# A decoder layer on one core: a 256/320 column split, the pool's four products in one group, and memory heads first in the out-projection

## The chip, the cores and the metric

The kernel runs on one core of one Trainium2 chip. The metric is the device time of one launch in microseconds (us), as the median of several runs. The engines are TensorE (PE, with its weight loads shown apart as PEld), VectorE (DVE), ScalarE (ACT), GpSimd (POOL) and SyncE (SP), which here only issues transfers. Each engine works through its own queue in order; where one needs another's result it waits on a semaphore.

## The reference

One decoder layer for 256 tokens of width 2048, in fp32:

```python
h = rms_norm(x, g_mix)
z = h @ w_in        # columns: pool 512 | q latent 512 | kv latent 256 | rope key 64 | memory query 512
y_pool = pool_mixer(z_pool, w_pool, pool_scale)
y_mla  = mla_mixer(z_q, z_kv, z_kr, ...)              # 8 heads, causal
y_mem  = memory_cross_attention(z_mq, mem, ...)       # 4 heads over 256 memory rows
x = x + concat([y_pool, y_mla, y_mem]) @ w_o
x = x + conv_glu_ffn(rms_norm(x, g_ffn), ...)         # inner width 5632
```

`pool_mixer` takes, in four groups of 128 channels, a causal mean over the last 2, 4, 8 and 16 tokens less the token itself, multiplies each group by its own 128x128 matrix in `w_pool`, and scales the columns.

## The kernel before

Weights are fp32 in DRAM and come in through SP's queue in pieces of up to 128x2048 (tile `wr`, three buffers, `load_w`). Each piece is split on chip into a high part (`wh`, a cast on ACT, line 98) and a residue (`wl`, a subtraction on DVE, line 99); activations are split in the same way (`split_act`, the high part on ACT, the residue on DVE). A product then is three products of halves: high with high, low with high, high with low. Two forms are used: `gemm_t` and its like (weights stationary, results by feature) and `gemm_n` (activations stationary, results by token, lines 173 to 175 in the profile). Small products, transposes, scores and the pool's matrices stay in plain fp32.

PSUM is held as two pools of four banks each, `psm` for the large products and `psa` for all else.

The order in the first part of the layer:

1. Memory keys and values: `mem @ w_mem_kv` (16 steps of k, `gemm_n`, lines 317 to 328). The chip's transfer engines are full here.
2. Memory queries and rope key: `xg @ [w_mq | w_kr]`, 576 columns, 16 steps of k. For each step and each of two blocks of 128 tokens the 576 columns go to two PSUM banks (`pss`, from `ps_aux`), 288 to each; `mq_done` copies them out, to `t` (512 columns) and `kr` (64).
3. Latents of q and kv (`gemm_z`, six of them), with the four memory heads between them; their outputs lie in `catm`, the memory heads' part of the concatenation.
4. Four pool groups (`pool_in(0)` to `pool_in(3)`), with `q_up` and `kv_up` (up-projections of queries, keys and values) between them.
5. `pool_mix`: on DVE the sliding sums (tiles `s4`, four steps that double the window) and the differences (line 575, into `zp`); then for each group one fp32 product with its matrix (line 577, a `psa` bank each) and a `split_act` from that bank into `cat`, the pool's and the MLA heads' part. The matrices come by one transfer on ACT's queue into `wp`, one of three rotating tiles `tok` (line 564).
6. `q_up(1)` and `kv_up(1)`, the last queries and the values. Then the out-projection: for each of four column blocks `n`, `out_part(0, n, pss, c)` takes for c = 0 the pool features (`cat`, k 0 to 3) and for c = 1 the memory heads (`catm`), a second round takes the MLA heads. `mla_steps` is called after each k of the first round and lays the MLA heads between the products: rotated keys first (`rope_keys`: a product on DVE into a `tok`, eight transposes on PE at line 688, four copies on DVE at line 693 into `qkv`), then scores (line 703), softmax, transposes, values.
7. The GLU, 44 pairs (lines 145 to 158), and the down-projection (lines 866 to 967).

The code is written in the order above, but a scheduler orders each engine's queue, save for instructions under `keep`, which stay as written among themselves. It also sets the semaphores: where a tile is written again, the writer waits for the readers of what stood in it, and for a PSUM tile this holds for the bank as a whole, whichever columns are touched.

Of the kernel before, what the change touches and what calls it, by code (L numbers as in the profile page):

```python
# [11 lines left out]
F32 = mybir.dt.float32  # L12
# [6 lines left out]
P = 128  # L19
T = 256  # L20
NT = 2
# [39 lines left out]
def layer(ctx, tc, xT_d, xn_d, memT_d, vec_d, tab_d, w_z_d, w_mqkr_d, w_q_d, w_kv_d, w_mem_d, w_pool_d, w_o_d,  # L61
          w_g_d, w_u_d, w_dn_d, out_d):
    nc = tc.nc
# [15 lines left out]
    def ps_aux():  # L79
        return psa.tile([P, 512], F32, tag="a", name=nm("psa"))  # L80
# [7 lines left out]
    def keep(ins, on=True):  # L88

        return tc.keep_in_program_order(ins) if on else ins  # L90
# [69 lines left out]
    def gemm_n(pss, hi, lo, act, k0, first, last, kept=False, by_span=False):  # L160

        nk, n = hi.shape[1], hi.shape[2]
        nj = len(pss[0])
        w = n // nj
        order = [(tt, j) for tt in range(NT) for j in range(nj)]
        if by_span:
            order.sort(key=lambda x: x[1])
        for i in range(nk):
            for tt, j in order:
                xh = act[:, k0 + i, tt * P:(tt + 1) * P]  # L170
                xl = act[:, k0 + i, T + tt * P:T + (tt + 1) * P]
                ps, o = pss[tt][j], slice(j * w, (j + 1) * w)
                keep(nc.tensor.matmul(ps, xh, hi[:, i, o], start=first and i == 0, stop=False), kept)  # L173
                keep(nc.tensor.matmul(ps, xl, hi[:, i, o], start=False, stop=False), kept)  # L174
                keep(nc.tensor.matmul(ps, xh, lo[:, i, o], start=False, stop=last and i == nk - 1), kept)  # L175

    def split_act(dst, src, scale=None, kept=False):


        h, l = (dst[:, 0], dst[:, 1]) if len(dst.shape) == 3 else (dst[:, 0:T], dst[:, T:2 * T])  # L180
        if scale is None:
            nc.scalar.copy(h, src)
            nc.vector.tensor_tensor(l, src, h.bitcast(F32), op=ALU.subtract)
        else:
            keep(nc.scalar.activation(h, src, AF.Copy, scale=scale), kept)
            keep(nc.vector.scalar_tensor_tensor(l, src, scale, h.bitcast(F32), op0=ALU.mult, op1=ALU.subtract), kept)
# [4 lines left out]
    def v(name, i=0):  # L191
        o = VOFF[name] + i
        return vec[:, o:o + 1]
# [16 lines left out]
    mp = mix.enter_context(tc.tile_pool(name="mix", bufs=1))  # L210
# [12 lines left out]
    def tok():  # L223
        return mp.tile([P, 512], F32, tag="tok", name=nm("tok"), bufs=3)
# [67 lines left out]
    ps = ps_aux()  # L292
# [24 lines left out]
    pss = [[ps_main()[:] for _ in range(2)] for _ in range(NT)]  # L317
    for c in range(KD // 2):
# [5 lines left out]
        for i in range(2):  # L324
            k = 2 * c + i
# [3 lines left out]
        if c % 2:  # L329
            h = slice(2 * c - 2, 2 * c + 2)  # L330
# [5 lines left out]
    ps = ps_aux()  # L336
# [54 lines left out]
        nc.vector.tensor_tensor(rx2, rx, rx, op=ALU.mult)  # L391


    NH = 288
    kr = mp.tile([P, NT, ROPE], F32, name="kr")
    fmq = sm(NT * XH)
    fmq3 = fmq.rearrange("p (t h) -> p t h", h=XH)
    pss = [[ps_aux()[:, :NH] for _ in range(2)] for _ in range(NT)]
    for c in range(KD // 2):
        raw = load_w(w_mqkr_d[c], 2 * 576)  # L400
        for i in range(2):
# [15 lines left out]
    def mq_done():  # L417

        x_rstd()
        for tt in range(NT):  # L420
            t = tok()
            nc.scalar.copy(t[:, 0:NH], pss[tt][0][:, :NH])
            nc.scalar.copy(t[:, NH:512], pss[tt][1][:, :512 - NH])
            nc.scalar.copy(kr[:, tt, :], pss[tt][1][:, 512 - NH:NH])
            head_sq(fmq3[:, tt], t[:].rearrange("p (h d) -> p h d", d=XD))
            nc.vector.tensor_scalar(fmq3[:, tt], fmq3[:, tt], rx2[:, tt:tt + 1], None, op0=ALU.mult)
            to_features(mqT, t, tt, XH, gqk[:, 1:2])
        rsqrt_(fmq, fmq, 1.0 / XD)
        for tt in range(NT):
            nc.vector.tensor_scalar(fmq3[:, tt], fmq3[:, tt], rx[:, tt:tt + 1], 1.0 / math.sqrt(XD),  # L430
                                    op0=ALU.mult, op1=ALU.mult)


        dx = tok()
        for tt in range(NT):
            nc.vector.tensor_scalar(dx[:, tt * P:(tt + 1) * P], identf[:], rx[:, tt:tt + 1], None, op0=ALU.mult)
        ps = ps_aux()
        nc.tensor.matmul(ps[:, 0:T], ones[:], dx[:, 0:T], start=True, stop=True)
        nc.scalar.copy(rxb[:], ps[:, 0:T])
# [73 lines left out]
    zl = mp.tile([P, 6, 2 * T], F32R, name="zl")  # L513
# [4 lines left out]
    for m in range(6):  # L518
# [3 lines left out]
        ps = ps_main()  # L522
# [3 lines left out]
        a = zs[:, m // 4, :]  # L526
# [23 lines left out]


    zp = mp.tile([P, 4, T], F32, name="zp")
    def pool_in(g):
        raw = load_w(w_z_d[6 + g], STG)
        ps = ps_main()
        gemm_z(ps, raw, lambda k: xg[:, k, :], lambda: mem_steps(6 + g), False) if g == 0 else gemm_t(
            ps, raw, 0, lambda k: xg[:, k, :], range(KD))
        half_add(zp[:, g, :], ps)
        nc.vector.tensor_tensor(zp[:, g, :], zp[:, g, :], rxb[:], op=ALU.mult)


    def pool_mix():
        wp = tok()
        nc.scalar.dma_start(wp[:], w_pool_d)
        cur, w = zp, 1
        for g in range(4):
            nxt = s4()
            nc.vector.tensor_copy(nxt[:, g:4, 0:w], cur[:, g:4, 0:w])
            nc.vector.tensor_tensor(nxt[:, g:4, w:T], cur[:, g:4, w:T], cur[:, g:4, 0:T - w], op=ALU.add)
            cur = nxt  # L570
            w *= 2
            s = cur[:, g, :]
            e = TAB["edge"][0] + 16 * g
            nc.vector.tensor_tensor(s[:, 0:16], s[:, 0:16], tab[:, e:e + 16], op=ALU.mult)
            nc.vector.scalar_tensor_tensor(zp[:, g, :], s, 1.0 / w, zp[:, g, :], op0=ALU.mult, op1=ALU.subtract)
            ps = ps_aux()
            nc.tensor.matmul(ps[:, 0:T], wp[:, g * P:(g + 1) * P], zp[:, g, :], start=True, stop=True)
            split_act(cat[:, g, :], ps[:, 0:T], v("pool_scale", g))


    qkv = big.tile([P, 32, T], F32, tag="act", name="qkv")
# [49 lines left out]
    def kv_up(n):  # L631
        raw = load_w(w_kv_d[n], STG)
        for h in range(2):
            pss = [[ps_main()[:]] for _ in range(NT)]
            hi, lo = split_w(raw, h * HS, HS)
            gemm_n(pss, hi[:].rearrange("p (k n) -> p k n", n=512), lo.rearrange("p (k n) -> p k n", n=512),
                   zl, 4, True, True)
            for tt in range(NT):
                ps = pss[tt][0]
                p3 = ps.rearrange("p (h d) -> p h d", d=128)  # L640
                if n == 1:
                    nc.scalar.activation(vv[:, tt, 4 * h:4 * h + 4, :], p3, AF.Copy, scale=skv[:, tt:tt + 1])
                    continue
                t = tok()
                t3 = t[:].rearrange("p (h d) -> p h d", d=NOPE)
                o = slice(tt * H + 4 * h, tt * H + 4 * h + 4)
                nc.scalar.copy(t[:], ps)
                head_sq(fk[:, o], t3)
                nc.vector.tensor_scalar(fk[:, o], fk[:, o], skv2[:, tt:tt + 1], sskr[:, tt:tt + 1],
                                        op0=ALU.mult, op1=ALU.add)  # L650
                rsqrt_(fk[:, o], fk[:, o], 1.0 / QK)
                nc.vector.tensor_scalar(fkn[:, o], fk[:, o], skv[:, tt:tt + 1], None, op0=ALU.mult)
                nc.vector.tensor_scalar(fkr[:, o], fk[:, o], rx[:, tt:tt + 1], None, op0=ALU.mult)
                nc.vector.tensor_tensor(t3, t3, fkn[:, o].unsqueeze(2).to_broadcast([P, 4, NOPE]), op=ALU.mult)
                to_features(knT[:, 4 * h:4 * h + 4], t, tt, 4, None, "v")
# [21 lines left out]
                                op0=ALU.mult, op1=ALU.mult)  # L677

    kv_up(1)

    def rope_keys():
        for tt in range(NT):
# [43 lines left out]
        if done[0] == 4 * H + 4:  # L726
            mla_heads[H - 1].values()

    def out_part(i, n, pss, c):

        raw = load_w(w_o_d[i, n, c], STG)
        for h in range(2):
            hi, lo = split_w(raw, h * HS, HS)
            w = [t.rearrange("p (k n) -> p k n", n=NN) for t in (hi[:], lo)]
            k = c * 4 + h * 2
            act, k = (cat, 4 + k) if i else (cat, k) if k < 4 else (catm, k - 4)
            for r in range(2):
                kept = i == 0 or n + c == 0
                gemm_n(pss, *(t[:, r:r + 1] for t in w), act, k + r, c + h + r == 0, c + h + r == 3, kept)
                if kept:  # L740
                    mla_steps()

# [5 lines left out]

    for n in range(4):
        pss = [[ps_main()[:]] for _ in range(NT)]  # L750
        for c in range(2):
            out_part(0, n, pss, c)
        out_add(n, pss)


# [21 lines left out]
    for n in range(4):  # L777
        pss = [[ps_main()[:]] for _ in range(NT)]
        for c in range(2):
            out_part(1, n, pss, c)  # L780
        out_done(n, pss)
        if n:
            turn(n - 1)
# [268 lines left out]
```

## Time and profile before

| | us |
|---|---|
| median of 3 runs | 1003.43 (1003.19 to 1003.74) |
| profiled span, first to last instruction | 1001.9 |
| PE busy | 996.0 |
| DVE busy | 767.7 |
| ACT busy | 587.0 |

The profiled execution has a span of 1001.9 us; the page gives no other time for it, and the runs' median lies 1.5 us above, for what is around the span. A row of the timeline gives the start and the length in us, the engine, the line, the operation, the tiles written and read (buffer numbers left out) and how many were merged; in brackets the engine's idle time before it and what ended it. Lengths of matmuls overlap, so their pace is read from start to start. An fp32 product of the pool shows as two records.

By place in the span: memory keys and values up to 50 us, memory queries and rope key 50 to 77, latents and memory heads to about 126, pool groups and up-projections to 177, then the out-projection.

### The profile page before, as it was taken

Reading aid. Unit: us, or ns where it says so; the run is one execution under the profiler, and the core shown is the slowest. Engines: PE = TensorE matmul, PEld = TensorE weight load, DVE = VectorE, ACT = ScalarE, POOL = GpSimd, SP = SyncE. Lnnn points to the kernel's source line nnn. Section 1 sums busy time; section 2 is a strip of 40 time slices with the busy share of each in tenths; the row PEclk is TensorE's granted clock in tenths of the full one; section 3 lists DMA queues with packets and bytes.
Section 4 is the critical chain, followed back from the end, with each engine's and each line's share of the span. In section 5 each row is a group of like instructions: output and inputs, shape, how many; then the busy total and the mean of one; then the engine's idle time right before and its main releaser. Section 6 shows DMA issues by size and latency. Waiting matters only on the chain.

```text
span 1001.9 us, 14016 instructions
## 1 busy us (share of the span) xinstructions
PE 996.0 (99%) x5338; PEld 857.8 (86%) x5338; DVE 767.7 (77%) x1160; ACT 587.0 (59%) x859; POOL 18.5 (2%) x39
## 2 busy tenths in 40 slices
PE   9999999999999999999999999999999999999998
PEld 7898888888888888888888888888888888888886
DVE  6778689855677767677767677777677898998997
ACT  7678666544576556555655565555565665545652
POOL 1010000000000000000000000000000000010000
PEclk9999999999999999999999999999999999999999
DMA  9867443433664555555555555555556655585651
GB/s 357 293 241 281 156 175 138 167 128 132 232 224 169 199 188 202 174 205 188 191 200 192 197 180 199 194 184 208 189 191 223 240 207 178 203 305 199 216 205 43
DMA packets 31764, 200.17 MB, mean 200 GB/s; under 512 B 3664, under 2 KB 4176, under 8 KB 9808
## 3 DMA queue, kind: packets, MB, share of 16 engines
q1 hardware_dynamic: 28512, 189.04, 52.8%
q0 software_dynamic: 2752, 9.44, 2.7%
q8 instruction: 42, 0.69, 0.3%
q10 hardware_dynamic: 432, 0.79, 0.2%
q14 instruction: 26, 0.21, 0.1%
HBM read 195.06 MB, written 4.19 MB: 199 GB/s over the span
## 4 chain that ended last, share of the span: by engine, by line
PE 99%; DVE 0%; issue 0%
PE psm L156 47%; PE psm L175 5%; PE psm L173 5%; PE psm L174 5%; PE psm L140 4%; PE psa L882 4%; PE psm L882 4%; PE psa L880 4%; PE psa L881 4%; PE psm L880 4%; PE psm L881 4%; PE psm L124 3%; PE psa L703 1%; PE psa L173 1%; PE psa L175 1%; PE psa L174 1%
## 5 line engine op out<-in xcount | busy, mean ns | idle before, releaser
L99 DVE TENSOR_TENSOR wl<-wr,wh 128x1024 fp32r<-128x1024 f32 (+2 forms) x338 | 390.5, 1170 | 133.7 <-ACT wh L98 76.0
L98 ACT CAST wh<-wr 128x1024 fp32r<-128x1024 f32 (+2 forms) x338 | 339.5, 1009 | 139.3 <-PE psm L156 55.4
L156 PE MATMUL psm<-h,wh 128*128 128x512 f32 x1376 | 320.1, 390 | 0.0
L156 PEld LDWEIGHTS psm<-h,wh 128*128 128x128 f32 x1376 | 255.1, 188 | 51.2
L156 PEld LDWEIGHTS psm<-h,wl 128*128 128x128 f32 x1376 | 163.8, 188 | 3.3
L156 PE MATMUL psm<-h,wl 128*128 128x256 f32 x1376 | 164.5, 277 | 0.0
L98 ACT CAST wh<-dn 128x1024 fp32r<-128x1024 f32 (+1 forms) x66 | 66.0, 1008 | 75.5 <-PE psa L881 35.1
L99 DVE TENSOR_TENSOR wl<-dn,wh 128x1024 fp32r<-128x1024 f32 (+1 forms) x66 | 75.0, 1164 | 15.8 <-ACT wh L98 15.8
L817 ACT ACTIVATE gc<-g,vec 128x256 f32<-128x256 f32 x44 | 26.5, 602 | 93.4 <-DVE g L815 93.4
L819 DVE SCALAR_TENSOR_TENSOR gc<-g,vec,gc 128x255 f32<-128x255 f32 x88 | 42.5, 483 | 33.0 <-ACT gc L817 31.4
L173 PE MATMUL psm<-wh,cat 128*128 128x512 f32 x96 | 38.2, 398 | 0.0
L175 PE MATMUL psm<-wl,cat 128*128 128x512 f32 x96 | 37.4, 390 | 0.0
L174 PE MATMUL psm<-wh,cat 128*128 128x512 f32 x96 | 37.4, 389 | 0.0
L881 PE MATMUL psa<-wh,aT 128*128 128x512 f32 x88 | 34.3, 390 | 0.0
L880 PE MATMUL psa<-wh,aT 128*128 128x512 f32 x88 | 34.3, 389 | 0.0
L881 PE MATMUL psm<-wh,aT 128*128 128x512 f32 x88 | 34.3, 389 | 0.0
L880 PE MATMUL psm<-wh,aT 128*128 128x512 f32 x88 | 34.2, 389 | 0.0
L882 PE MATMUL psa<-wl,aT 128*128 128x512 f32 x88 | 33.9, 389 | 0.0
L882 PE MATMUL psm<-wl,aT 128*128 128x512 f32 x88 | 33.9, 389 | 0.0
L809 ACT COPY g<-psm 128x256 f32<-128x256 f32 x44 | 16.5, 375 | 27.7 <-PE psm L156 27.7
L881 PE MATMUL psm<-wh,aS 128*128 128x512 f32 x77 | 30.0, 390 | 0.0
L881 PE MATMUL psa<-wh,aS 128*128 128x512 f32 x77 | 30.0, 390 | 0.0
(238 smaller groups left out, 1424.2 us busy)
## 6 DMA issues: line engine op xcount, KB each, us to landing
wr<-in_w_g SPq DMA_DIRECT2D x44, 1024.0 KB, 4.8
wr<-in_w_u SPq DMA_DIRECT2D x44, 1024.0 KB, 4.8
wr<-in_w_dn SPq DMA_DIRECT2D x33, 1024.0 KB, 4.9
wr<-in_w_o SPq DMA_DIRECT2D x16, 1024.0 KB, 4.8
dn<-in_w_dn SPq DMA_DIRECT2D x11, 1024.0 KB, 4.8
wr<-in_w_z SPq DMA_DIRECT2D x10, 1024.0 KB, 6.7
wr<-in_w_mem SPq DMA_DIRECT2D x6, 1024.0 KB, 8.4
wr<-in_w_mqkr SPq DMA_DIRECT2D x8, 576.0 KB, 5.2
```

The lines of the kernel that those rows point to most:

```text
L98: keep(nc.scalar.copy(hi[:, c:e], raw[:, o + c:o + e]), kept)
L99: keep(nc.vector.tensor_tensor(lo[:, c:e], raw[:, o + c:o + e], hi[:, c:e].bitcast(F32), op=ALU.subtract), kept)
L124: keep(nc.tensor.matmul(out, w, m, start=first and c + i == 0 and not low, stop=last and c == cs[-1] and i == len(kc) - 1 and low == (c // ...
L140: keep(nc.tensor.matmul(o, parts[k // nk][low][:, i * P:(i + 1) * P], m, start=k == 0 and low == low_first, stop=k == KD - 1 and low != lo ...
L156: nc.tensor.matmul(o, parts[k // nk][low][:, i * P:(i + 1) * P], m, start=k == 0 and low == (s == 1), stop=k == KD - 1 and low == (s == 0) ...
L173: keep(nc.tensor.matmul(ps, xh, hi[:, i, o], start=first and i == 0, stop=False), kept)
L174: keep(nc.tensor.matmul(ps, xl, hi[:, i, o], start=False, stop=False), kept)
L175: keep(nc.tensor.matmul(ps, xh, lo[:, i, o], start=False, stop=last and i == nk - 1), kept)
L819: nc.vector.scalar_tensor_tensor(gc[:, d:T], g[:, 0:T - d], v(w, f), gc[:, d:T], op0=ALU.mult, op1=ALU.add)
L880: nc.tensor.matmul(ps, a[0], b[0], start=first, stop=False)
L881: nc.tensor.matmul(ps, a[1], b[0], start=False, stop=False)
L882: nc.tensor.matmul(ps, a[0], b[1], start=False, stop=last)
```

## The change

- The 576 columns go as 256 and 320 instead of twice 288; `gemm_n` takes the widths from the PSUM tiles. The copies in `mq_done` become 256 + 256 and 64.
- `pool_mix` keeps the sums and differences. The four products move into a function of their own, `pool_out`, that is called after `kv_up(1)`. Two products share one `psa` bank, in its two halves; the products are under `keep`, and so are those of the last half of `kv_up`. The matrices get a tile of their own, `wp`.
- In the first column block of the out-projection the memory heads (c = 1) come before the pool features (c = 0).

```diff
@@ gemm_n
-        w = n // nj
+        at = [0]
+        for p in pss[0]:
+            at.append(at[-1] + p.shape[1])
...
-                ps, o = pss[tt][j], slice(j * w, (j + 1) * w)
+                ps, o = pss[tt][j], slice(at[j], at[j + 1])
@@ memory queries and rope key
-    NH = 288
+    NH = (256, 320)
-    pss = [[ps_aux()[:, :NH] for _ in range(2)] for _ in range(NT)]
+    pss = [[ps_aux()[:, :n] for n in NH] for _ in range(NT)]
...
-            nc.scalar.copy(t[:, 0:NH], pss[tt][0][:, :NH])
-            nc.scalar.copy(t[:, NH:512], pss[tt][1][:, :512 - NH])
-            nc.scalar.copy(kr[:, tt, :], pss[tt][1][:, 512 - NH:NH])
+            nc.scalar.copy(t[:, 0:256], pss[tt][0])
+            nc.scalar.copy(t[:, 256:512], pss[tt][1][:, 0:256])
+            nc.scalar.copy(kr[:, tt, :], pss[tt][1][:, 256:320])
@@ pool
+    wp = mp.tile([P, 4 * P], F32, name="wp")
...
     def pool_mix():
-        wp = tok()
         nc.scalar.dma_start(wp[:], w_pool_d)
...
+    def pool_out():
+        for a in range(2):
             ps = ps_aux()
-            nc.tensor.matmul(ps[:, 0:T], wp[:, g * P:(g + 1) * P], zp[:, g, :], start=True, stop=True)
-            split_act(cat[:, g, :], ps[:, 0:T], v("pool_scale", g))
+            for g in (2 * a, 2 * a + 1):
+                o = ps[:, (g % 2) * T:(g % 2 + 1) * T]
+                keep(nc.tensor.matmul(o, wp[:, g * P:(g + 1) * P], zp[:, g, :], start=True, stop=True))
+                split_act(cat[:, g, :], o, v("pool_scale", g))
@@ kv_up
-                   zl, 4, True, True)
+                   zl, 4, True, True, n + h == 2)
...
     kv_up(1)
+    pool_out()
@@ out-projection
-    def out_part(i, n, pss, c):
+    def out_part(i, n, pss, c, o):
...
-                gemm_n(pss, *(t[:, r:r + 1] for t in w), act, k + r, c + h + r == 0, c + h + r == 3, kept)
+                gemm_n(pss, *(t[:, r:r + 1] for t in w), act, k + r, o + h + r == 0, o + h + r == 3, kept)
...
-        for c in range(2):
-            out_part(0, n, pss, c)
+        for o in range(2):
+            out_part(0, n, pss, o if n else 1 - o, o)
```

What the scheduler made of it is seen in the queues. PE at the end of `kv_up(1)`, before; names carry their buffer numbers, and the brackets name the semaphores that a row waits for (of DVE, of ACT, of PE itself, of a transfer). L577 are the pool's products, L266 transposes of queries, L173 to L175 products of `kv_up`.

```order
L173 MATMUL psm_301_1885<-wh_303_1887,zl_839 128x512 [waits Activation_49]
L577 MATMUL psa_280_1785<-zp_1289,tok_274_1760 128x256 [waits DVE_49]
L174 MATMUL psm_301_1885<-wh_303_1887,zl_839 128x512
L175 MATMUL psm_301_1885<-wl_304_1888,zl_839 128x512
L577 MATMUL psa_282_1794<-zp_1289,tok_274_1760 128x256 [waits DVE_49]
L266 MATMUL psa_292_1839<-identf_68,tok_290_1834 128x128 x4
L266 MATMUL psa_295_1850<-identf_68,tok_293_1845 128x128 [waits Activation_49]
L266 MATMUL psa_295_1850<-identf_68,tok_293_1845 128x128 x3
L173 MATMUL psm_302_1886<-wh_303_1887,zl_839 128x512
```

The third and fourth product stand between products of `kv_up`, each with its own bank. The same place after; lines are 2 to 8 higher, L584 are the pool's products, L696 the transposes of the rope keys, L175 to L177 the out-projection.

```order
L177 MATMUL psm_297_1870<-wl_299_1872,zl_839 128x512
L584 MATMUL psa_300_1889<-zp_1289,wp_1290 128x256 [waits DMAHW1_49,DVE_49]
L584 MATMUL psa_300_1889<-zp_1289,wp_1290 128x256 [waits DVE_49]
L584 MATMUL psa_301_1896<-zp_1289,wp_1290 128x256
L696 MATMUL psa_308_1919<-identf_68,tok_307_1917 128x128 [waits PE_49]
L696 MATMUL psa_308_1919<-identf_68,tok_307_1917 128x128 x3
L696 MATMUL psa_310_1928<-identf_68,tok_309_1926 128x128 [waits Activation_49]
L696 MATMUL psa_310_1928<-identf_68,tok_309_1926 128x128 x3
L584 MATMUL psa_301_1896<-zp_1289,wp_1290 128x256 [waits DVE_49]
L175 MATMUL psm_302_1903<-wh_305_1907,catm_838 128x512
```

The products stand behind `kv_up(1)`, with the eight transposes of the rope keys between the third and the fourth. The second product's wait on DVE is for the read of the first out of `psa_300`, the fourth's for the read of the third out of `psa_301`. The eight transposes of queries have moved ahead, between the products of `kv_up(1)`, four at a time.

DVE's queue around its reads of these banks (L186 before, L188 after), before:

```order
L671 TENSOR_TENSOR small_82<-small_82 128x16 [waits DVE_49]
L684 TENSOR_TENSOR tok_310_1919<-krr_1292,small_82 128x512 [waits DMAHW1_49,PE_49]
L186 SCALAR_TENSOR_TENSOR cat_1759<-psa_282_1794,vec_67,cat_1759 128x256 [waits Activation_49]
L673 TENSOR_SCALAR small_82<-small_82 128x8 [waits DVE_49]
L673 TENSOR_SCALAR small_82<-small_82 128x8
L684 TENSOR_TENSOR tok_312_1928<-krr_1292,small_82 128x512 [waits PE_49]
L206 RECIPROCAL small_82<-small_82 128x16 [waits Activation_49]
L99 TENSOR_TENSOR wl_315_1944<-wr_307_1907,wh_314_1943 128x1024
L676 TENSOR_SCALAR small_82<-small_82 128x8 [waits DVE_49]
L676 TENSOR_SCALAR small_82<-small_82 128x8
L99 TENSOR_TENSOR wl_324_1996<-wr_322_1993,wh_323_1995 128x1024 [waits DMAHW2_49]
```

and after:

```order
L692 TENSOR_TENSOR tok_309_1926<-krr_1293,small_82 128x512 [waits PE_49]
L99 TENSOR_TENSOR wl_312_1942<-wr_304_1905,wh_311_1941 128x1024
L208 RECIPROCAL small_82<-small_82 128x16 [waits Activation_49]
L99 TENSOR_TENSOR wl_321_1994<-wr_319_1991,wh_320_1993 128x1024 [waits DMAHW2_49,PE_49]
L683 TENSOR_SCALAR small_82<-small_82 128x8 [waits DVE_49]
L683 TENSOR_SCALAR small_82<-small_82 128x8
L188 SCALAR_TENSOR_TENSOR cat_1760<-psa_300_1889,vec_67,cat_1760 128x256 [waits Activation_49]
L99 TENSOR_TENSOR wl_328_2033<-wr_319_1991,wh_327_2032 128x1024 [waits PE_49,Activation_49]
L188 SCALAR_TENSOR_TENSOR cat_1760<-psa_300_1889,vec_67,cat_1760 128x256 [waits Activation_49]
L188 SCALAR_TENSOR_TENSOR cat_1760<-psa_301_1896,vec_67,cat_1760 128x256 [waits Activation_49]
L701 COPY qkv_1291<-psa_308_1919 64x4x128 [waits PE_49,Pool_49]
```

Before, three of the four reads stand ahead of the first row shown; after, all four stand behind the residues of two more weight pieces (`wl_312` and `wl_321`), with a third (`wl_328`) between the first and the second. The transfer of the matrices, which was the 183rd entry of ACT's queue, is now the ninth, ahead of a cast of memory weights.

More of the change, by code (lines that the diff above doesn't have):

```diff
@@ L779, in layer @@
         for c in range(2):
-            out_part(1, n, pss, c)
+            out_part(1, n, pss, c, c)
         out_done(n, pss)
```

## Prediction

> **What bounds the kernel now.** I read the page first, then the chain of waits by engine, then the timeline of TensorE and VectorE around the three places that the diff touches.
>
> ```profile
> span 1001.9 us, 14016 instructions
> PE 996.0 (99%) x5338; PEld 857.8 (86%) x5338; DVE 767.7 (77%) x1160; ACT 587.0 (59%) x859; POOL 18.5 (2%) x39
> ...
> PE 99%; DVE 0%; issue 0%
> ```
>
> TensorE (PE) is the bound from end to end: busy for 996.0 of 1001.9 us, and the chain that ended last is 99% PE. So two things alone can move the time: how long PE needs for its own products, and how long PE waits. Work on VectorE (DVE), ScalarE (ACT) or a queue counts only where it makes PE wait. The profiled span is 1001.9 us and the median of the runs 1003.43 us; I take the 1.5 us between them as fixed and add my difference to the median.
>
> **Part 1, the column split.** The stage of memory queries and rope key issues three groups of 64 matmuls of 288 columns, 192 in all, so 96 pairs of neighbouring pieces.
>
> ```profile
> L173 PE MATMUL psa<-wh,xg 128*128 128x288 f32 x64 | 19.0, 298 | 0.0
> ```
>
> The mean of 298 ns is from start to end and overlaps the next one; what counts is the distance from start to start.
>
> ```profile
> 53.02 0.29 PE L173 MATMUL psa<-wh,xg 128*128 128x288 f32 x1
> ...
> 56.62 0.29 PE L173 MATMUL psa<-wh,xg 128*128 128x288 f32 x1
> ...
> 402.81 3.83 PE L156 MATMUL psm<-h,wl 128*128 128x256 f32 x32
> 406.47 7.44 PE L156 MATMUL psm<-h,wh 128*128 128x512 f32 x32
> 413.75 3.82 PE L156 MATMUL psm<-h,wl 128*128 128x256 f32 x32
> ```
>
> The first two rows are 27 matmuls apart: 3.60/27 = 133.3 ns for 288 columns. The next three give (406.47 - 402.81)/32 = 114.4 ns for 256 and (413.75 - 406.47)/32 = 227.5 ns for 512. So 32 columns fewer than 288 save 18.9 ns, while 224 more cost 94.2, or 0.42 ns a column: there is a step just above 256. 320 columns have no row. On the line from 288 to 512 they take 133.3 + 32 x 0.42 = 146.8 ns, and the pair 261.2 instead of 266.7 ns: 5.5 ns x 96 = **0.53 us gained**, on PE's path, since PE runs there without gaps. The ends: 133.3 ns (if the step is a round-up that 320 still fits under) gives 1.8 us gained; 152.3 ns (if the 18.9 ns come back on the other piece) gives nothing. I take the line, since 288 is the nearest row. The copies out (288+224+64 columns, now 256+256+64) run on ACT beside PE's next products and cost nothing.
>
> [...]
>
> **Part 2, the pool's products.** Before, they lie one by one between the products of the value up-projection; each has a PSUM bank of its own.
>
> ```profile
> 163.19 0.39 PE L173 MATMUL psm<-wh,zl 128*128 128x512 f32 x1
> ...
> 168.18 0.39 PE L174 MATMUL psm<-wh,zl 128*128 128x512 f32 x1
> 168.60 0.67 PE L577 MATMUL psa<-zp,tok 128*128 128x256 f32 x2
> ...
> 169.34 0.39 PE L173 MATMUL psm<-wh,zl 128*128 128x512 f32 x1
> ...
> 170.26 0.59 PE L577 MATMUL psa<-zp,tok 128*128 128x256 f32 x2
> ...
> 170.93 0.39 PE L175 MATMUL psm<-wl,zl 128*128 128x512 f32 x1
> ...
> 174.11 1.03 PE L266 MATMUL psa<-identf,tok 128*128 128x128 f32 x8
> ...
> 175.22 0.39 PE L174 MATMUL psm<-wh,zl 128*128 128x512 f32 x1
> ...
> 177.03 0.39 PE L173 MATMUL psm<-wh,cat 128*128 128x512 f32 x1
> ```
>
> 163.19 to 168.18 holds 22 products: 0.227 us each. From 170.26 to 170.93 there is one product of the pool and one such product, so a pool product takes 0.67 - 0.23 = 0.44 us; eight transposes take 1.11 - 0.23 = 0.88 us (110 ns each). Back to back a product cannot be much under 0.43, so grouping by itself saves some 0.01 us each. The first product waits: 168.18 to 169.34 is 1.16, less 0.45 and 0.44 leaves 0.27 us, because its input ends late on DVE. Behind the up-projection that input is long ready, so this 0.27 us goes.
>
> What comes instead: two products now share one PSUM bank, and PE's second product waits until DVE has read the first out of it (the waits in the order above; `split_act` ends on DVE). So the question is when DVE gets there.
>
> ```profile
> 163.79 0.42 DVE L510 TENSOR_TENSOR zp<-hadd,psm 128x256 f32<-128x256 f32 x1 [0.90 <-ACT hadd L509]
> ...
> 165.92 1.22 DVE L99 TENSOR_TENSOR wl<-wr,wh 128x1024 fp32r<-128x1024 f32 x1
> 167.06 0.17 DVE L574 TENSOR_TENSOR s<-s,tab 128x16 f32<-128x16 f32 x1
> ...
> 168.08 0.42 DVE L575 SCALAR_TENSOR_TENSOR zp<-s,zp 128x256 f32<-128x256 f32 x1
> ...
> 170.63 0.48 DVE L186 SCALAR_TENSOR_TENSOR cat<-psa,vec,cat 128x256 fp32r<-128x256 f32 x1
> 171.03 0.17 DVE L574 TENSOR_TENSOR s<-s,tab 128x16 f32<-128x16 f32 x1
> ...
> 173.25 0.69 DVE L260 TENSOR_REDUCE small<-hsq 128x4 f32<-128x512 f32 x1
> 174.08 0.48 DVE L186 SCALAR_TENSOR_TENSOR cat<-psa,vec,cat 128x256 fp32r<-128x256 f32 x1
> ...
> 177.93 1.22 DVE L99 TENSOR_TENSOR wl<-wr,wh 128x1024 fp32r<-128x1024 f32 x1
> ...
> L186 DVE SCALAR_TENSOR_TENSOR cat<-psa,vec,cat 128x256 fp32r<-128x256 f32 x4 | 1.9, 484 | 0.1
> ```
>
> DVE is full here: from 163.79 to 177.93 it runs 14.14 us with one pause of 0.2 (before 174.08). After the change the same run stands ahead of the first `cat` operation, less four `cat` operations (0.40 each, 170.63 to 171.03), less the pause, plus one weight residue more, of 1.14 (165.92 to 167.06): 14.14 - 1.60 - 0.2 + 1.14 = 13.48. Its start, 163.79, hangs on PE and stays. So the first `cat` operation starts at 177.27 and ends, 0.48 later, at 177.75; PE starts 0.10 after such an end (168.08 + 0.42 to 168.60), at **177.85**.
>
> PE would be ready much sooner: 163.19 + 48 x 0.227 (the products up to the group) + 0.88 (the eight transposes of queries, now among them) + 0.43 (the first product) = 175.4. It waits **2.45 us**. From there: the second product, with the 0.07 that a product after a wait takes longer (the 0.67 of the first row against 0.59), to 178.35; the third to 178.8; the eight transposes of rope keys, pulled in here, to 179.68. The fourth product waits again, for DVE's read of the third: on DVE the residue for 1.14 follows at 177.67, to 178.8; ACT reads the second product from 178.6 (its end trails by 0.2, the 0.59 over the 0.43) for 0.48 (row below), DVE reads it from 179.1 for 0.40, then the third, to 180.0. PE goes on at 180.1: **0.42 us** more. The fourth product ends at 180.6, and the out-projection starts. Before, it started at 177.03 without the rope transposes, that is 177.91 with their 0.88. Part 2 costs 180.6 - 177.9 = **2.7 us**, its removed wait included. Its ends: 0.3 us gained if DVE were never late, and 3.2 if both queues run 0.25 later than I place them; the rows are those of this very stretch, so I keep 2.7.
>
> ```profile
> 169.58 0.48 ACT L185 ACTIVATE cat<-psa,vec 128x256 fp32r<-128x256 f32 x1
> ...
> 179.10 2.85 DVE L693 COPY qkv<-psa 64x512 f32<-64x512 f32 x4
> ...
> 182.22 0.39 PE L703 MATMUL psa<-qkv,mqT 128*128 128x128 f32 x2
> ```
>
> **Part 3, memory heads first.** PE does the same products in another order, at no cost. It is cover: pool features are then first needed 24 products (5.4 us) and the first scores after 180.6, and DVE has them by 182. Without it the first product at 180.6 would wait. The four rope copies (2.85 us, done at 181.95 for a score at 182.22) move too: they start at 180.0 with a 0.40 `cat` operation among them and end near 183.3, while the scores now come at 180.6 + 18 x 0.227 = 184.7. No wait follows.
>
> **The pool weights' transfer** moves from ACT's queue near 157 us to its ninth place at the start.
>
> ```profile
> 9.64 1.05 ACT L98 CAST wh<-wr 128x1024 fp32r<-128x1024 f32 x1 [0.97 <-DMA wr<-in_w_mem]
> ...
> 17.60 1.06 ACT L98 CAST wh<-wr 128x1024 fp32r<-128x1024 f32 x1 [0.62 <-DMA wr<-in_w_mem]
> ...
> 22.58 0.39 PE L173 MATMUL psm<-wh,mg 128*128 128x512 f32 x1
> ...
> 10.00:15.00 5.00, 4.96 (x22) 3.79 (x21) 3.76 (x5) 4.23 (x6) 0.68 (x1) 1.00 1.05 428
> ```
>
> The issue fits in ACT's 0.97 us of waiting before 9.64. The engines are full then (428 GB/s), so 256 KB delay what follows by 0.6 us; the cast at 17.60 feeds PE at 22.58, so 3.9 us lie between. Cost nothing; with that cover gone, 0.6.
>
> **Sum:** 2.7 - 0.53 = +2.15 us, so 1003.43 + 2.15 = **1005.6 us**. A change of 0.2% (2.0 us) is about what a measurement here can tell, so I stand hardly beyond it.
>
> **Rivals.**
> - Split without a gain (152 ns for 320): +2.7, 1006.1 us. For it: no row for 320; against: the step above 256. [...]
> - 320 at 288's price: 2.7 - 1.8 = +0.9, 1004.3 us. For it: a step exists; against: 512 lies on a slope.
> - Not slower: DVE reads the shared banks in time, so that no wait replaces the one removed. It decides at 175.4: if the first `cat` operation ends before that, 2.35 us sooner than I place it, 0.3 + 0.53 are gained: 1002.6 us. For it: today DVE reads the first product 2.0 us after its start (168.60 to 170.63) while PE goes on. Against it: ahead of that operation stand two residues and the rope keys' work, and DVE's run has no pause to skip.
> - The clock. At the start PE runs slow after idling:
>
> ```profile
> 1.05 4.30 PE L294 MATMUL psa<-ones 128*128 128x128 f32 x20 [1.05 <-DVE eps L201]
> ```
>
> 4.30/20 is 215 ns for 128 fp32 columns, where later ones take 110: half speed for about 4 us, though the granted clock reads 1.00. If 2.45 us of waiting brings that back, another 4.3 us at half speed add 2.1: 1007.7 us. Against it: no wait of this length is in the trace. [...]
>
> **How the numbers follow.** The forecast has 0.66, with a range of its own of 1005.1 to 1006.0, six tenths of it beyond +0.2%. Split without gain 0.12, 320 at 288's price 0.08, DVE in time 0.07, clock 0.07. Slower: 0.40 + 0.12 + 0.07 = 0.59. Same: 0.26 + 0.08 + most of 0.07, less a little for a gain beyond 0.2% that I cannot place: 0.37. Faster: 0.04. The range 1004.2 to 1006.4 holds the forecast and both prices of 320, and leaves out DVE in time and the clock (0.14).
>
> **What would show it.** Right: PE waits about 2.4 us before the second pool product and 0.4 before the fourth, both ended by the `cat` operation on DVE; 256 columns at 114 ns and 320 at 147 start to start; no wait at the first scores or the first pool features of the out-projection. Wrong: no PE wait in the group, 320 columns at 133 or over 152 ns, matmuls at half speed after the wait, or a new wait in the first 20 us.

## The result and the profile after

The changed kernel takes 1007.21 us (median of 7 runs, 1006.17 to 1007.90), the kernel before 1003.56 (7 runs, 1003.19 to 1003.88): ratio 1.0034, interval 1.0024 to 1.0043. It is slower by 3.65 us, where 2.15 were predicted. Its runs fall in two groups: three at 1006.17 to 1006.20 us with a mean granted clock of 0.999, and four at 1007.21 to 1007.90 with 0.997 to 0.998. The profiled execution is of the lower group: 1006.17 us with a span of 1004.4, so 1.8 us lie around the span. For the kernel before it is the same (runs of 1003.55 us have a span of 1001.8).

The page of the changed kernel:

```profile
span 1004.4 us, 14015 instructions
PE 996.2 (99%) x5338; PEld 858.4 (85%) x5338; DVE 767.0 (76%) x1160; ACT 586.9 (58%) x859; POOL 18.5 (2%) x39
...
PE 98%; DVE 1%; issue 0%; ACT 0%
```

PE has the same work (996.2 us against 996.0), and a per cent of the chain has gone from PE to DVE. The timeline of PE shows where (start, length, then the row's work; the bracket is idle time and what ended it):

```profile
174.89 0.60 PE L584 MATMUL psa<-zp,wp 128*128 128x256 f32 x2
177.67 1.13 PE L584 MATMUL psa<-zp,wp 128*128 128x256 f32 x4 [2.19 <-DVE cat L188]
178.64 1.04 PE L696 MATMUL psa<-identf,tok 128*128 128x128 f32 x8
179.89 0.70 PE L584 MATMUL psa<-zp,wp 128*128 128x256 f32 x2 [0.21 <-DVE cat L188]
180.24 0.58 PE L175 MATMUL psm<-wh,catm 128*128 128x512 f32 x1
```

The first pool product is through at 174.89 + 0.43 = 175.32, the second starts at 177.67: PE stands for 2.35 us. (The bracket says 2.19, since it counts from the modelled end of the product ahead, not from when the next could have started.) The eight transposes end at 178.64 + 8 x 0.11 = 179.52, and the fourth product waits 0.37 more. VectorE in the same place:

```profile
177.14 0.48 DVE L188 SCALAR_TENSOR_TENSOR cat<-psa,vec,cat 128x256 fp32r<-128x256 f32 x1
177.53 1.22 DVE L99 TENSOR_TENSOR wl<-wr,wh 128x1024 fp32r<-128x1024 f32 x1
178.92 0.92 DVE L188 SCALAR_TENSOR_TENSOR cat<-psa,vec,cat 128x256 fp32r<-128x256 f32 x2 [0.17 <-ACT cat L187]
```

The read of the first product ends at 177.62, and PE goes on 0.05 us later; the third product's read, behind a residue and the second product's, ends the second wait.

For the sum, landmarks of both kernels: the first product of the memory queries, the first one behind them, the first of the last query up-projection, the first of the GLU. Before (the third landmark, 163.19, stands in the prediction):

```profile
50.15 0.38 PE L173 MATMUL psa<-wh,xg 128*128 128x288 f32 x1
...
76.79 0.87 PE L140 MATMUL psm<-xg,wh 128*128 128x512 f32 x3
...
287.90 2.07 PE L124 MATMUL psm<-h,wh 128*128 128x512 f32 x8
```

After, with three rows of the split:

```profile
50.05 0.37 PE L175 MATMUL psa<-wh,xg 128*128 128x256 f32 x1
...
50.94 0.28 PE L175 MATMUL psa<-wh,xg 128*128 128x256 f32 x1
...
51.30 0.31 PE L175 MATMUL psa<-wh,xg 128*128 128x320 f32 x1
...
51.74 0.28 PE L175 MATMUL psa<-wh,xg 128*128 128x256 f32 x1
...
76.68 0.86 PE L140 MATMUL psm<-xg,wh 128*128 128x512 f32 x3
...
163.07 0.39 PE L175 MATMUL psm<-wh,zl 128*128 128x512 f32 x1
...
290.45 2.07 PE L124 MATMUL psm<-h,wh 128*128 128x512 f32 x8
```

The stage of memory queries lasts 26.63 us after and 26.64 before: the split gains nothing. From 163.07 to the GLU it is 127.38 us against 124.71: **+2.67 us**, all in the part of the pool's products. The rest of the span differs by less than 0.15. So the profiled execution, and the lower group of runs, is explained. What puts four of seven runs another 1.0 to 1.7 us higher does not show in this trace.

### The profile page after: what moved, and what is told of

Same layout as the page of the kernel before. It is cut to its first block, busy times and chain, and to the rows that moved or that the text cites. A ratio compares the mean times of both kernels' runs of the same rounds, so it can differ in the third digit from the quotient of the medians.

```text
span 1004.4 us, 14015 instructions
## 1 busy us (share of the span) xinstructions
PE 996.2 (99%) x5338; PEld 858.4 (85%) x5338; DVE 767.0 (76%) x1160; ACT 586.9 (58%) x859; POOL 18.5 (2%) x39
## 4 chain that ended last, share of the span: by engine, by line
PE 98%; DVE 1%; issue 0%; ACT 0%
PE psm L156 47%; PE psm L175 5%; PE psm L176 5%; PE psm L177 5%; PE psm L140 4%; PE psa L890 4%; PE psm L890 4%; PE psa L888 4%; PE psa L889 4%; PE psm L888 4%; PE psm L889 4%; PE psm L124 3%; PE psa L711 1%; PE psa L175 1%; PE psa L177 1%; PE psa L176 1%
## 5 line engine op out<-in xcount | busy, mean ns | idle before, releaser
L175 PE MATMUL psm<-wh,cat 128*128 128x512 f32 x96 | 38.1, 397 | 0.0
L177 PE MATMUL psm<-wl,cat 128*128 128x512 f32 x96 | 37.4, 390 | 0.0
```

## Experiments

The theory: the two waits for a shared PSUM bank cost 2.67 us in each run, and in some runs the idling also brings TensorE's clock down for a while. The rivals: another part of the change costs (the early transfer, the order, the split), or the upper group has nothing to do with the idling.

### A bank for each product

```diff
         for a in range(2):
-            ps = ps_aux()
             for g in (2 * a, 2 * a + 1):
-                o = ps[:, (g % 2) * T:(g % 2 + 1) * T]
+                o = ps_aux()[:, 0:T]
```

> The four pool products stay in one group behind the value up-projection, but each gets a PSUM bank of its own. Theory W (the loss is TensorE's two waits for the shared banks, and what the clock does after the longer one): both waits are gone, about 2.8 us of the profiled span with them; span 1001.6, runs at 1003.1 to 1003.4 us, all with the granted clock of the kernel before (1.000), none in a second cluster. Rival R (something else in the change costs, such as the early transfer, the split or the order): the waits go, but runs stay at 1004.4 or above, or still fall in two clusters 1.0 to 1.7 us apart.

Measured: 1003.54 us (11 runs, 1003.02 to 1003.70), one group; ratio to the kernel before 0.9999, interval 0.9990 to 1.0007. PE's timeline:

```profile
162.94 0.39 PE L175 MATMUL psm<-wh,zl 128*128 128x512 f32 x1
...
174.77 1.89 PE L583 MATMUL psa<-zp,wp 128*128 128x256 f32 x8
176.31 0.58 PE L175 MATMUL psm<-wh,catm 128*128 128x512 f32 x1
...
287.42 2.07 PE L124 MATMUL psm<-h,wh 128*128 128x512 f32 x8
```

All four products run without a pause, and both the waits and the upper group are gone, although the split, the early transfer, the group and the new order are all still there. The loss is therefore the shared banks. The trace gains 0.23 us on the kernel before from the up-projection to the GLU (124.48 against 124.71), about the wait of 0.27 that the prediction saw there. The runs do not show that gain: 1003.1 to 1003.4 us were expected, and the profiled run, at 1003.02, is the fastest of the eleven. This is the best version of the study, and it equals the kernel before.

### The even split put back

```diff
-    NH = (256, 320)
+    NH = (288, 288)
```

(with the copies of `mq_done` as before)

> The changed kernel with the columns split as before, 288 and 288; the rest of the change is kept. Theory P (start to start a product takes (columns + 32)/2.4 ns here, so that both splits cost the pair 266.7 ns): the stage of memory queries lasts as long as in the changed kernel within 0.1 us, spans 1004.4 and 1005.4 to 1006.1 as there, two clusters of runs as there. Rival (the step on record: 256 columns at 114.4 ns, 320 at 146.8): the stage is 0.53 us longer and spans begin at 1004.9.

Measured: 1006.79 us (5 runs: 1006.08, 1006.45, 1006.79, 1007.55, 1007.55), ratio 1.0033, interval 1.0020 to 1.0046, close to the changed kernel. Its stage of memory queries takes 26.65 us (50.18 to 76.83), against 26.63 with 256 and 320. Here the profiled execution fell in the upper group (span 1005.8), and its timeline shows what that is:

```profile
175.09 0.60 PE L584 MATMUL psa<-zp,wp 128*128 128x256 f32 x2
177.86 1.83 PE L584 MATMUL psa<-zp,wp 128*128 128x256 f32 x4 [2.18 <-DVE cat L188]
179.48 1.91 PE L696 MATMUL psa<-identf,tok 128*128 128x128 f32 x8
181.19 0.79 PE L584 MATMUL psa<-zp,wp 128*128 128x256 f32 x2
181.62 0.58 PE L175 MATMUL psm<-wh,catm 128*128 128x512 f32 x1
```

The same wait of 2.34 us, but what follows it is slow: the second and third product take 177.86 to 179.48, 1.62 us instead of 0.97 (177.67 to 178.64 above), and 179.48 to 181.19 is 214 ns for each of the eight transposes instead of 110. The wait before the fourth product is gone, because PE now comes later than VectorE. In windows (from and to, length, PE busy with its count, granted clock, DMA share, GB/s):

```profile
174.00:178.00 4.00, 1.82 (x9) 1.00 0.26 47
178.00:179.00 1.00, 1.00 (x3) 0.57 0.99 418
179.00:180.00 1.00, 1.00 (x5) 0.50 1.06 434
...
181.00:182.00 1.00, 1.00 (x5) 0.72 0.98 418
182.00:186.00 4.00, 4.00 (x19) 1.00 0.29 119
```

The granted clock is 0.50 from shortly after the wait until about 181.6. Against the changed kernel's profile this run is 1.21 us longer between the same landmarks (163.26 to 291.85).

A stretch of 3.41 us at half clock takes 1.7 of some 1005 us, or 0.0017, off the mean granted clock of a run. So that mean tells the groups apart: 0.999 or 1.000 below, 0.997 or 0.998 above. The run at 1006.79 us lies between the groups with 0.999, so it had no such stretch; what it lost is not shown.

### A shorter wait

ScalarE copies the first product of each bank to SBUF, and VectorE splits it from there:

```diff
+                if g % 2 == 0:
+                    nc.scalar.copy(spare[:, a, :], o)
+                    o = spare[:, a, :]
                 split_act(cat[:, g, :], o, v("pool_scale", g))
```

> The changed kernel, but the first product of each shared bank is first copied to SBUF by ScalarE and split from there, so that the bank comes free when ScalarE has read it instead of VectorE: TensorE's wait should be about 1.0 us instead of 2.35, and about 0.25 instead of 0.38. Theory W (a short wait costs its length alone, a wait beyond some 2 us sometimes brings the slow clock as well): 1.5 us less than the fast cluster of the changed kernel, 1004.5 to 1004.8 us, all runs with a clock of 0.999 or more and within 0.4 us. Rival C (any wait of a microsecond can bring the slow clock): two clusters, the upper at 1005.7 or more with a clock of 0.998.

Measured: 1004.48 us (11 runs, 1004.25 to 1004.74, where 1004.5 to 1004.8 were expected), one group, clock 0.999 or 1.000; ratio 1.0009, interval 1.0000 to 1.0018.

```profile
175.01 0.60 PE L586 MATMUL psa<-zp,wp 128*128 128x256 f32 x2
176.28 1.13 PE L586 MATMUL psa<-zp,wp 128*128 128x256 f32 x4 [0.67 <-ACT spare L588]
```

The wait is 176.28 - 175.44 = 0.84 us, and 0.84 is about what the runs are above those with a bank each (0.94). In these eleven runs a wait this short costs its length and no more.

### A longer wait

Six more copies of the first product out of its bank, on VectorE:

```diff
+                for _ in range(6 if g == 0 else 0):
+                    nc.vector.tensor_copy(spare[:], o)
                 split_act(cat[:, g, :], o, v("pool_scale", g))
```

> The changed kernel with six more copies of the first product out of its shared bank on VectorE (their result is not used), which lengthen TensorE's wait before the second product to about 6 us. Theory W (after so long a wait the products run at half speed for about 4 us): every run has the lower clock (0.997 or less), the trace shows products 454 ns apart instead of 227 behind the wait, and the time is 6.4 + 0.7 us of waits and some 1 to 2 us for the slow products above own banks: 1011.3 to 1012.5 us, in one cluster. Rival (the waiting is all; the lower clock of some runs has another cause): products 227 ns apart behind the wait and 1010.2 us.

Measured: 1012.79 us (4 runs, 1012.02 to 1013.56), clock 0.994 to 0.996 in all; ratio 1.0094, interval 1.0079 to 1.0110.

```profile
174.85 0.60 PE L586 MATMUL psa<-zp,wp 128*128 128x256 f32 x2
181.61 2.08 PE L586 MATMUL psa<-zp,wp 128*128 128x256 f32 x4 [6.16 <-DVE cat L188]
183.47 1.27 PE L700 MATMUL psa<-identf,tok 128*128 128x128 f32 x5
```

A wait of 6.33 us brings the half clock in all four runs, as their granted clock shows. In the profile the second and third pool products take 181.61 to 183.47, 1.86 us instead of 0.97. By the records of the clock (last section) it had begun already during the wait, at 178.48, and that part of it cost nothing. Two of the four runs lie above the range expected, by 0.6 and 1.1 us; no trace was kept of these, and why is open.

### The same delay without the idling

Five more products of 256 fp32 columns, with no use of their result, in the wait:

```diff
                 split_act(cat[:, g, :], o, v("pool_scale", g))
+                if g == 0:
+                    fill = ps_aux()[:, 0:T]
+                    for i in range(5):
+                        keep(nc.tensor.matmul(fill, wp[:, 0:P], zp[:, 0, :], start=True, stop=True))
```

> The changed kernel with five extra products of 256 fp32 columns laid into TensorE's long wait (their result is not used), 5 x 0.43 = 2.15 of its 2.35 us. The second pool product still cannot start before VectorE has read the first, so the delay is the same and only the idling is gone. Theory W (the upper cluster of the changed kernel is the half-speed clock that follows the idling): all runs in the lower cluster, 1006.0 to 1006.4 us, profiled span 1004.3, no stretch with a granted clock of 0.5 behind the wait. Rival (the upper cluster comes from elsewhere, or from the delay itself): runs at 1007.2 to 1007.9 remain.

Measured: 1006.35 us (9 runs, 1005.96 to 1006.49), one group; ratio 1.0025, interval 1.0015 to 1.0035.

```profile
174.72 0.60 PE L584 MATMUL psa<-zp,wp 128*128 128x256 f32 x2
175.15 2.32 PE L589 MATMUL psa<-zp,wp 128*128 128x256 f32 x10
177.50 1.13 PE L584 MATMUL psa<-zp,wp 128*128 128x256 f32 x4
...
179.72 0.70 PE L584 MATMUL psa<-zp,wp 128*128 128x256 f32 x2 [0.21 <-DVE cat L188]
```

The second product starts 2.35 us behind the end of the first as before (177.50 - 175.15), so the delay of the lower group stays, and the upper group is gone. Useless work on the engine that is the bound brings the median from 1007.21 to 1006.35 us. The upper group is the idling, and not the delay.

With one extra product instead of five (`range(1)`):

> As warm_wait with one extra product instead of five: the same delay, but TensorE idles 1.9 us instead of 2.35. The traces so far show the granted clock change only on a grid of 3.41 us (174.08 and 822.61 us at full clock are 51 and 241 of it), half clock after a grid cell with 2.34 us of idling, and none after a cell with about 2.0. Theory G (a cell must be idle for more than some 2.0 us): all runs at 1006.0 to 1006.4. Rival (about 1 to 1.9 us in a cell suffice): runs above 1007 remain, fewer than in the changed kernel.

Measured: 1006.27 us (10 runs, 1005.99 to 1006.40), one group; ratio 1.0026, interval 1.0016 to 1.0035.

```profile
175.57 0.59 PE L589 MATMUL psa<-zp,wp 128*128 128x256 f32 x2
177.92 1.13 PE L584 MATMUL psa<-zp,wp 128*128 128x256 f32 x4 [1.76 <-DVE cat L188]
```

The upper group is missing here too: 1.92 us of idling (177.92 - 176.00) brought it in none of ten runs, 2.35 us in four of seven.

### A wait of 3 us

As the longer wait, with `range(2 if g == 0 else 0)`:

> As wait_plus6 with two extra copies instead of six: TensorE idles about 3.1 us. Theory G: a cell of 3.41 us then holds more than 2.3 us of the idling in most positions of the grid, so most runs (at least 6 in 10) have the half-speed stretch: those at 1007.9 to 1008.6, the others at 1006.9. [...]

Measured: 1008.03 us (5 runs: 1007.19, 1007.87, 1008.03, 1008.17, 1008.48), ratio 1.0042, interval 1.0029 to 1.0055. In its profile the wait is 178.36 - 175.37 = 2.99 us:

```profile
174.94 0.60 PE L586 MATMUL psa<-zp,wp 128*128 128x256 f32 x2
178.36 1.13 PE L586 MATMUL psa<-zp,wp 128*128 128x256 f32 x4 [2.82 <-DVE cat L188]
179.33 1.56 PE L700 MATMUL psa<-identf,tok 128*128 128x128 f32 x8
180.68 1.12 PE L586 MATMUL psa<-zp,wp 128*128 128x256 f32 x2
181.24 0.99 PE L175 MATMUL psm<-wh,catm 128*128 128x512 f32 x1
```

The two products right behind the wait still run at full speed (0.97 us), and the clock falls only among the transposes (1.56 instead of 1.04 us), 1.3 us after PE went on. So it isn't set by when the wait ends. Four of five runs lie at 1007.87 or above, as the grid theory had it. None lies at 1006.9, where that theory put the runs without the stretch. The lowest, at 1007.19, is nearest to it and has a clock of 0.999, so it had no half-speed stretch; the other four have 0.997 or 0.998.

### Pool features first again

```diff
-            out_part(0, n, pss, o if n else 1 - o, o)
+            out_part(0, n, pss, o, o)
```

> The changed kernel with part 3 undone: the first column block of the out-projection takes the pool's features before the memory heads again. The step on record (memory heads first is cover; without it the first product of the out-projection would wait for the pool's features): a third wait of TensorE of 0.5 to 1.5 us behind the group, 1006.7 us and above even in the lower cluster. Rival N (by the rows of the changed kernel the first features are ready at 177.6 and the fourth group's, needed 18 products or 4.1 us after the start at 180.4, by 181.7): no wait, the same two clusters as the changed kernel, 1006.1 and 1007.2 to 1007.9.

Measured: 1007.28 us (5 runs: 1006.15, 1006.21, 1007.28, 1007.44, 1007.74), ratio 1.0032, interval 1.0020 to 1.0045. No third wait:

```profile
179.73 0.70 PE L584 MATMUL psa<-zp,wp 128*128 128x256 f32 x2 [0.21 <-DVE cat L188]
180.08 0.58 PE L175 MATMUL psm<-wh,cat 128*128 128x512 f32 x1
```

The order of the out-projection changes nothing that these five runs show, in the lower group or in the upper.

## Why the prediction was wrong, and where it was right

- **The direction and the main term were right.** Part 2 was put at +2.7 us and measured 2.67: a wait of 2.35 us (predicted 2.45) ended by the `cat` operation that starts at 177.14 (predicted 177.27), and one of 0.37 (0.42). Walking VectorE's queue op by op gave that. The first product behind each wait takes some 0.11 us longer (the second and third together 0.97 instead of 0.86), where I had 0.07; with that, 2.35 + 0.37 + 0.22 - 0.27 = 2.67. The removed wait of 0.27 us was real too: with a bank each, 0.23 comes back.
- **Part 1 was mis-sized: a gain of 0.01 us instead of 0.53.** 320 columns were placed well (146.8 predicted; 51.30 to 51.74 holds three, 146.7 ns each). 256 was not: 50.94 to 51.30 gives 120 ns, where I took 114.4 from the GLU. So the pair costs 266.7 ns in both splits, and the rival "split without a gain" holds, but at the other end: 256 was dear, not 320. The step above 256 that I read from two stages does not exist within this one. In it 120, 133.3 and 146.7 ns for 256, 288 and 320 columns lie on one line of 0.417 ns a column, so both pairs are equal. Why 256 columns take 114 ns in the GLU and 120 here was not tried.
- **The clock was the step that failed.** The sum put the half clock at nothing, and four of seven runs pay for it. With part 1 at nothing, the sum is 1003.56 + 2.67 = 1006.2 us, where the lower group lies; the median is a microsecond higher. I had this rival, with the right mechanism, and gave it 0.07, on the ground that no wait of this length was in the trace. Waits of 2.34 and 2.99 us were enough in the profiles of the even split and of the 3 us wait. Its size was taken too large as well: 2.1 us, from 4.3 us at half speed. It is 1.0 to 1.7: the stretch is 3.41 us, so 1.7 at most, and the 0.37 us wait for the fourth product vanishes in it. Of the 1.6 us between forecast and median, about 1.0 is the clock, 0.5 the split, and 0.1 the kernel before, which came out at 1003.56 instead of 1003.43. In which group the median of seven runs falls is chance: about half of the runs lie in each, and a median of 1006.2 us would have hidden this step.
- **Part 3 as cover was wrong without consequence.** I wrote that without memory heads first the first product would wait. The first features are ready by then, and the fourth group's are needed 18 products later; pool features first cost nothing (180.08 in that run's timeline, right behind the group).
- **The early transfer** cost nothing, as predicted: the stage behind the full transfer engines (1.04 of their time and 420 GB/s from 10 to 20 us) begins at 50.05 us against 50.15.
- **The span and the median**: both kernels have 1.8 us around the span. The 1.5 that I took compared an execution with the median of others; it did not enter the difference.

## What to carry to other kernels

Two products that share a PSUM bank tie TensorE to the reader of the first one, where, as here, the bank is guarded as a whole (the second product, in the other half, stood for 2.35 us). When that reader's queue is full, give each product its own bank: here that gave back all that the sharing had cost (1003.54 against 1007.21 us), while the grouping itself gained nothing that the runs show. Price a wait of TensorE not by its length alone: where it passes about 2 us (here 1.92 us brought the half clock in none of ten runs, 2.35 in four of seven), add the half clock behind it, with a chance, and look at several runs and not at one profile, which showed only the lower group here. Take the price of a shape from rows of the stage in which it will run: 256 columns took 114 ns in the GLU and 120 among the memory queries.

## What the runs showed of the hardware

In these six traces the records of the granted clock change only on a grid. From the first record on, the stretches are (start, length, share, in us; the end of the launch left out):

```
changed kernel    6.60 996.69 1.0
pool first        5.32 996.69 1.0
own banks         5.14 996.69 1.0
even split        4.07 174.08 1.0 | 178.15 3.41 0.5 | 181.56 822.61 1.0
wait of 3 us      5.61 174.08 1.0 | 179.69 3.41 0.5 | 183.10 822.61 1.0
wait of 6 us      4.40 174.08 1.0 | 178.48 6.83 0.5 | 185.31 822.61 1.0
```

All lengths are multiples of 3.413 us (51, 1, 2, 241, 292), and the first boundary lies elsewhere in each execution. No record stands for what is ahead of it, so the 1.00 that the windows give for the half-speed products of the first 4 to 6.6 us says nothing (in the changed kernel 20 products of 128 fp32 columns take (5.47 - 1.05)/20 = 221 ns each there, against 110 for such a product later). What seems to decide is how much of one such cell TensorE idled. In the even split, the cell that ends at 178.15 holds all 2.34 us of the wait, and the clock halves; in the 3 us wait, the cell that ends at 179.69 holds 178.36 - 176.28 = 2.08, or 61% of the cell, and it halves. In the changed kernel's profile, the cell from 173.85 to 177.26 holds 1.94, and it stays; with pool first the largest share is 1.52, and with one extra product it can never be over 1.92. The end of the launch, where TensorE has no more work, agrees. With a bank each, the last product starts at 996.13 and takes 0.23; the cell that ends at 998.42 then holds 2.06 us of idling, and the clock stays until 1001.83. With pool first, the last product starts at 999.25, the cell that ends at 1002.02 holds 2.54, and the clock falls there. So by these few traces the limit, as an estimate between the 2.06 us that left the clock up and the 2.08 that halved it, lies at about 2.07 us of idling in a cell, counted from when the next product could have started; counted from the modelled ends of the products it lies between 1.90 and 2.08. With 2.07, a wait of 2.35 us trips it in (3.41 + 2.35 - 4.14)/3.41 = 0.48 of the positions of the grid. The runs above 1007 us are 9 of the 17 of the three kernels with that wait (4 of 7, 2 of 5, 3 of 5), and these nine are the ones with a clock of 0.997 or 0.998.
